# Later landings in the order of the instructions: 2.5 and 2.1 behind the shared bus, not 1.8 and 1.1

## The chip, the cores and the metric

The kernel runs on one core of a Trainium2 chip. The core has a matrix engine (PE in the profile, its weight loads PEld), a vector engine (DVE), a scalar engine (ACT), GpSimd (POOL), and a queue that only issues DMAs (SP). Each has a queue of its own that is worked off in the order in which the program was written; semaphores hold an instruction back until its data are there. The metric is the device time of one execution in microseconds (us). Before the change the median of three runs is 2048.77 us (2047.79 to 2051.46).

## What is computed

One step of a one-layer streaming encoder, for a prompt of 1024 tokens and 8 samples of 16 new tokens each, 1152 tokens together, with 1024 channels:

```python
h = rmsnorm(x)
qa, ka, va, qi, ki, wi, qb, kb, vb, gb, bb, ab, ga, gbr = split(h @ w_in)
# A: an indexer picks top-k keys for each query, then softmax attention with a relative bias
oa = dsa(qa, qi, wi, k_all, v_all, ki_all, topk, rel_bias)
# B: short causal convolution, then the gated delta rule in chunks
ob = rmsnorm(gated_delta(conv(qb), conv(kb), conv(vb), g, beta, state)) * silu(gb)
x = x + (sigmoid(ga) * (oa @ w_proj_a) + sigmoid(gbr) * (ob @ w_proj_b)) @ w_out
u_gate, u_val = split(rmsnorm(x) @ w_up)
x = x + (gelu(causal_dwconv(u_gate)) * u_val) @ w_down
x = x + sigmoid(rmsnorm(x) @ w_ple_gate) * (p @ w_ple)
y = rmsnorm(x)
```

The samples attend to a cache of 256 past keys each beside their new ones, and carry on a delta-rule state and two convolution states. All these states are outputs too.

## The kernel before

**The work.** Activations lie with channels on the partitions and tokens along the free axis, in three blocks of 384 tokens. Every product with a weight is made of three matmuls: activations and weights are split into a high part (`H`, `wh`) and a low part (`L`, `wl`), and `wh`·`H`, `wh`·`L` and `wl`·`H` are added up in PSUM. A dense job (`_Job`) is one tile of 128 output channels: its weight tile is loaded (`wr`), split (`weights`, `part`), multiplied block by block into a bank (`dense`), and evacuated (`evac`).

**The stages.**

1. *Mixers.* `norm1`, then the dense projections of `w_in`. In between go the indexer (`indexer`), the search for the top-k threshold (`topk_rows`, on ACT and DVE), the local part of the delta rule (`gdn_local`), its scan over the chunks (`gdn_scan`), the prompt's attention (`attention`, three workers) and that of the samples (`samples`). `jpp` and `jb` are dense jobs for `w_ple` and `w_proj_b` that run in the same stage.
2. *Merge.* `ja` (`w_proj_a`), which needs the attention of prompt and samples, and `jo` (`w_out`).
3. *Up-projection* in 22 tiles (`_Up`), with seven half-size products in place of eight, convolution, gelu, product.
4. *Down-projection* in the same manner, the gate of the per-layer embedding (`jd`), the last norm.

**What sets the order.** The order of all queues is made by a planner in the program, `_Driver`. Each piece of work is a generator, a thread. It yields what it needs next: an engine (`PE`, `ACT`, `DVE`, `POOL`, `SP`), an event of another thread, a buffer of a bank of buffers (`_Banks`), or `DMA`, the landing of its own transfers. The planner holds a clock for each engine and a time for each thread. In `run` it takes, again and again, the thread that can start first (then the one of the smallest number for its priority) and lets it issue its next instructions. So the planned times appear nowhere in the program but as the order of the instructions in the queues. `dense` has priority 9, the last: dense matmuls go where nothing else can start earlier.

`note` advances the clocks by a cost that `cost` gives for each operation. A DMA (engine `SP`) takes 0.46 us of SP's clock, its transfer is put behind all others on one shared bus (`self.bus`, from 0.2 us after the issue), and the thread's landing time `th.dma` is the bus's time plus a constant, one for loads (source in DRAM) and one for stores. The transfer's own time is 0.05 us plus, for each row, 0.0025 us or its bytes over 360 GB/s, whichever is more. DMAs that ACT issues for an evacuation (`own`) are noted as SP's too.

The landing time is read at four places: a thread that yields `DMA` goes on at that time (`_start`); `give` marks a buffer free not before it; `stored` sets an event at it; and threads for a landing (`arrival`, `landed`, `down_split`) are handed it. The real wait is a semaphore that is set when the transfer has landed, whatever the planner thought; a wait that the planner does not know of, such as one for a tile that is used again with no bank around it, is kept by semaphores alone.

**The threads that the prediction speaks of.**

- `gdn_chain` (two of them) goes through 8 chunks of the prompt. For each it loads `x` and `r`, yields `DMA`, and makes some matmuls with DVE steps between them. `gdn_norm` goes through the chunks behind it: load `sg`, transpose, yield `DMA`, multiply, store to `obT`.
- `samples` starts after `gdn_scan` has ended. `attn_cache` loads for each of 8 batches a selector (`x` from `selM` into an `evo` buffer) and then four tiles of cached keys (`skr`), each time: take one of two buffers, issue, yield `DMA`. `attn_samples` (two of them, four batches each) splits each key tile (`skH`, `skL`), multiplies, takes the softmax (`sz`), multiplies by the values (`sv`), and after four batches by the new values (`svN`, with `szn`) and stores to `oaT`.
- `merge_loads` loads `oaT` and `obT` back into `L` and splits them into `H` and `L`, as inputs of `ja` and `jb`. The third block of `ja` waits for the store of the samples (`sdone`).
- `mixers` ends with `drv.run(*self.samples(s3), *ev, self.jb[-1].done)`: the merge's threads are made only after samples, attention and `jb` have been placed.
- `evo` is a bank of four buffers of 128x384, used by most evacuations, by attention's outputs and value loads, by the samples, and for the gates that `jb` loads ahead of each block (`pre_gate`).

Of the kernel before, what the change touches and what calls it, by code (L numbers as in the profile page):

```python
# [87 lines left out]
class _Driver:  # L88
# [33 lines left out]
    def note(self, e, cost, port=False, load=False):  # L122
        th = self.cur
        if th.eng == e and cost < 0.1:
            cost += self.OWN[e]
        s = max(self.clk[e], th.t if th.eng in (e, None) else th.t + self.LAT)
        if port:
            s = max(s, self.port[POOL if e == DVE else DVE])
            self.port[e] = s + cost
        self.clk[e] = s + cost  # L130
        if e == SP:
            self.bus = max(self.bus, s + 0.2) + cost
            self.clk[e] = s + 0.46
            th.dma = max(th.dma, self.bus + (1.8 if load else 1.1))
        else:
            th.t, th.eng = s + cost, e

# [3418 lines left out]
```

## Time and profile before

| | |
|---|---|
| median of three runs | 2048.77 us |
| lowest and highest | 2047.79, 2051.46 us |
| the profiled execution | 2047.44 us, its span 2045.6 us |
| mean granted clock of the matrix engine | 0.996 |
| busy: PE, DVE, ACT, POOL | 2009.0, 1530.1, 1024.2, 650.1 us |
| DMA, mean over the span | 172 GB/s |

The profile's span runs from the first to the last instruction of the program; the time of the execution has 1.84 us around it. A row of instructions names engine, operation, and output <- inputs by the program's tile names; buffer numbers are left out, so `evo` is any of the four. All instructions bear the line L192, that of the helper which records them, so the tile names tell them apart. In the list of waits a row has who waited, for what, us in total, times, and the longest.

### The profile page before, as it was taken

What the parts mean: (1) busy time and instruction counts of PE and PEld (TensorE: products, weight loads), DVE (VectorE), ACT (ScalarE), POOL (GpSimd) and SP (SyncE); (2) the same over time, 40 slices, a digit from 0 to 9 for tenths busy, and PEclk for the clock granted to TensorE, in tenths of its full rate; (3) what the DMA queues carried; (4) which work ended last, traced back from release to release, by engine and by line L of the source; (5) the groups of instructions that cost most, each with busy time, mean ns of one, the idle gap of its engine ahead of it and who ended that gap; (6) DMA issues with size and microseconds to landing.
All of it is one profiled execution on the core that took longest, in us unless ns stands there. A gap on an engine that the chain in (4) does not pass through costs nothing.

```text
span 2045.6 us, 37985 instructions
## 1 busy us (share of the span) xinstructions
PE 2009.0 (98%) x13440; PEld 1961.5 (96%) x13440; DVE 1530.1 (75%) x3708; ACT 1024.2 (50%) x2061; POOL 650.1 (32%) x871
## 2 busy tenths in 40 slices
PE   7999999999999999999999999999999999999998
PEld 6899999999999998989999999999999999999998
DVE  7278989988664777778655788787788786657797
ACT  5267667656644555576423344333343354434454
POOL 2244543432223434454354322111221210112322
PEclk9999999999999999999999999999999999999999
DMA  7443356766528574477575433434465366656463
GB/s 277 115 126 97 91 193 199 221 194 175 155 78 247 171 220 143 143 232 218 174 241 168 148 120 122 151 118 156 154 210 193 131 221 221 213 164 209 150 198 127
DMA packets 264014, 352.02 MB, mean 172 GB/s; under 512 B 43324, under 2 KB 207504, under 8 KB 263696
## 3 DMA queue, kind: packets, MB, share of 16 engines
q1 hardware_dynamic: 241024, 323.11, 50.5%
q10 hardware_dynamic: 22800, 26.49, 3.8%
q8 instruction: 106, 1.74, 0.4%
q14 instruction: 84, 0.69, 0.1%
HBM read 241.07 MB, written 110.08 MB: 172 GB/s over the span
## 4 chain that ended last, share of the span: by engine, by line
PE 88%; DVE 3%; DMA 3%; issue 1%; ACT 1%; SPq 0%; POOL 0%; ACTq 0%; DVEq 0%; POOLq 0%
PE up L192 36%; PE acc L192 35%; PE at L192 7%; PE dn L192 5%; PE gd L192 3%; PE ix L192 1%; DMA ppT<-evo 1%; PE rp L192 1%; DVE z L192 0%; DMA sg<-sgb 0%; SPq L192 0%; DMA obT<-sg 0%; DVE e L192 0%; DVE SC L192 0%; PE ixs L192 0%
## 5 line engine op out<-in xcount | busy, mean ns | idle before, releaser
L192 PE MATMUL acc<-H,wh 128*128 128x384 f32 (+1 forms) x1328 | 468.9, 353 | 3.1 <-ACT evo L192 3.0
L192 PE MATMUL acc<-H,wl 128*128 128x384 f32 (+1 forms) x1328 | 450.1, 339 | 0.5 <-POOL wl L192 0.5
L192 PE MATMUL acc<-L,wh 128*128 128x384 f32 (+1 forms) x1328 | 449.7, 339 | 0.0
L192 POOL TENSOR_TENSOR wl<-wr,wh 128x256 fp32r<-128x256 f32 (+1 forms) x255 | 220.4, 886 | 447.6 <-ACT wh L192 388.6
L192 PEld LDWEIGHTS acc<-H,wh 128*128 128x128 f32 x1328 | 250.4, 189 | 10.2 <-ACT evo L192 4.1
L192 PE MATMUL up<-B,wh 128*128 128x288 f32 x1272 | 257.1, 296 | 0.0
L192 PEld LDWEIGHTS acc<-L,wh 128*128 128x128 f32 x1328 | 250.6, 189 | 3.3
L192 PEld LDWEIGHTS acc<-H,wl 128*128 128x128 f32 x1328 | 249.9, 188 | 2.2 <-POOL wl L192 1.0
L192 PE MATMUL up<-T,wh 128*128 128x288 f32 x1012 | 243.4, 295 | 0.0
L192 PEld LDWEIGHTS up<-B,wh 128*128 128x128 f32 x1272 | 204.1, 188 | 0.0
L192 PE MATMUL up<-B,wl 128*128 128x288 f32 x636 | 187.9, 295 | 0.0
L192 PEld LDWEIGHTS up<-T,wh 128*128 128x128 f32 x1012 | 174.2, 188 | 0.1
L192 ACT CAST wh<-wr 128x1024 fp32r<-128x1024 f32 (+3 forms) x133 | 113.1, 851 | 116.8 <-PE acc L192 42.7
L192 POOL TENSOR_TENSOR ssq<-ssq,sqs 128x384 f32<-128x384 f32 (+1 forms) x69 | 70.5, 1024 | 166.7 <-ACT sqs L192 160.0
L192 PEld LDWEIGHTS up<-B,wl 128*128 128x128 f32 x636 | 119.4, 188 | 0.0
L192 ACT ACTIVATE ja<-SC,cola 128x768 bf16<-128x768 f32 (+2 forms) x93 | 96.8, 1041 | 25.4 <-DVE cola L192 19.1
L192 ACT CAST wh<-s 128x512 fp32r<-128x512 f32 x88 | 52.5, 619 | 102.7 <-PE up L192 97.0
L192 ACT COPY u<-up 128x576 f32<-128x576 f32 x64 | 40.9, 640 | 102.5 <-PE up L192 102.1
L192 PE MATMUL up<-T0L,wh 128*128 128x288 f32 x296 | 87.4, 295 | 0.3 <-DVE T0L L192 0.3
L192 DVE TENSOR_TENSOR wl<-s,wh 128x512 fp32r<-128x512 f32 x75 | 56.6, 762 | 41.3 <-ACT wh L192 40.9
L192 PE MATMUL up<-T0H,wh 128*128 128x288 f32 x296 | 87.4, 295 | 0.0
L192 PE MATMUL up<-T0H,wl 128*128 128x288 f32 x296 | 87.1, 294 | 0.0
(537 smaller groups left out, 5302.4 us busy)
## 6 DMA issues: line engine op xcount, KB each, us to landing
wr<-in_w_in SPq DMA_DIRECT2D x47, 512.0 KB, 3.9
AT<-fv SPq DMA_DIRECT2D x22, 576.0 KB, 3.1
wr<-in_w_up SPq DMA_DIRECT2D x22, 512.0 KB, 4.5
gates<-evo ACTq DMA_DIRECT2D x48, 192.0 KB, 3.3
xs<-in_w_down SPq DMA_DIRECT2D x48, 192.0 KB, 3.5
S<-xs SPq DMA_DIRECT2D x48, 192.0 KB, 4.0
qkv<-evo SPq DMA_DIRECT2D x36, 192.0 KB, 3.6
T<-AT SPq DMA_DIRECT2D x11, 576.0 KB, 3.9
```

The costliest lines, as they stand in the source:

```text
L192: r = f(*a, **k)
```

## The change

The two constants behind the bus become 2.5 us for a load and 2.1 us for a store, where they were 1.8 and 1.1. Nothing else is touched: no cost, no buffer, no thread, no instruction.

```diff
@@ -131,7 +131,7 @@
         if e == SP:
             self.bus = max(self.bus, s + 0.2) + cost
             self.clk[e] = s + 0.46
-            th.dma = max(th.dma, self.bus + (1.8 if load else 1.1))
+            th.dma = max(th.dma, self.bus + (2.5 if load else 2.1))
         else:
             th.t, th.eng = s + cost, e
```

## The prediction

> **What bounds the kernel now.** I read the page first, then the stretches of the span, then what the PE queue waited for.
>
> ```profile
> span 2045.6 us, 37985 instructions
> PE 2009.0 (98%) x13440; PEld 1961.5 (96%) x13440; DVE 1530.1 (75%) x3708; ACT 1024.2 (50%) x2061; POOL 650.1 (32%) x871
> PE 88%; DVE 3%; DMA 3%; issue 1%; ACT 1%; SPq 0%; POOL 0%; ACTq 0%; DVEq 0%; POOLq 0%
> ...
> 800.00:900.00 100.00, 93.79 (x629) 89.12 (x627) 71.00 (x218) 62.53 (x145) 49.90 (x74) 1.00 0.61 180
> 900.00:1000.00 100.00, 97.24 (x668) 92.60 (x667) 80.36 (x265) 66.82 (x167) 46.72 (x81) 1.00 0.66 201
> 1000.00:1020.00 20.00, 20.00 (x135) 19.97 (x134) 9.37 (x24) 4.78 (x12) 6.54 (x10) 1.00 0.62 188
> 1020.00:1040.00 20.00, 20.00 (x115) 20.00 (x114) 6.79 (x13) 4.34 (x8) 5.89 (x7) 1.00 0.87 273
> 1040.00:1200.00 160.00, 159.66 (x945) 159.19 (x944) 110.32 (x185) 63.08 (x126) 70.63 (x60) 1.00 0.52 164
> 1200.00:1900.00 700.00, 700.00 (x5282) 699.78 (x5281) 534.51 (x914) 288.30 (x473) 123.26 (x167) 1.00 0.52 172
> 1900.00:2045.60 145.60, 139.87 (x878) 139.06 (x876) 115.23 (x240) 71.78 (x124) 40.47 (x37) 0.97 0.48 158
> ```
>
> In the stretches the first pair is the window and its length, then busy time (and count) of PE, weight loads, DVE, ACT, POOL, then the granted clock and DMA. TensorE is the bound, at the full clock. The order of its queue can win at most 2045.6 - 2009.0 = 36.6 us, and from 1000 to 1900 us there is nothing to win: 0.3 us of idle time in all. Idle time lies in the mixers, where small products of attention and of the delta rule share the queue with the dense projections. That is where a planner's idea of a DMA's landing matters, because there it decides whether a small product or a dense one goes next. What PE waited for, over the whole span:
>
> ```profile
> PE ac L192 <- ACT H L192: 6.7, 1, 6.7
> PE at L192 <- DVE sg L192: 3.7, 2, 2.3
> PE acc L192 <- ACT evo L192: 3.0, 2, 1.9
> PE at L192 <- DMA evo<-vTs: 2.2, 2, 1.5
> ...
> PE gd L192 <- DMA vc<-qkv: 1.2, 1, 1.2
> ...
> PE at L192 <- DMA x<-qkv: 1.0, 1, 1.0
> ```
>
> The first is the start, before any matmul. The three that name a DMA are loads which came after the point where the order had put their product. The two behind `sg` belong with them: in 795 to 825 us DVE sat 3.0 us for the load of `sg` and PE 2.3 us for DVE.
>
> ```profile
> DVE sg L192 <- DMA sg<-sgb: 3.0, 1, 3.0
> ...
> PE at L192 <- DVE sg L192: 2.3, 1, 2.3
> ```
>
> **The change, part by part.** No instruction is added or removed. Every work thread that yields DMA is put back into the order 0.7 us later behind a load and 1.0 us later behind a store, and so is a buffer that is given back after its store. The instructions, their buffers and their semaphores stay; only places in the five queues move. What was planned and what was measured (KB each, median from issue to landing):
>
> ```profile
> gates<-evo ACTq DMA_DIRECT2D x48, 192.0 KB, 3.3
> evo<-gates SPq DMA_DIRECT2D x24, 192.0 KB, 2.4
> pbT<-evo SPq DMA_DIRECT2D x24, 192.0 KB, 2.7
> skr<-in_ckT SPq DMA_DIRECT2D x32, 128.0 KB, 2.3
> sg<-sgb SPq DMA_DIRECT2D x9, 256.0 KB, 2.8
> obT<-sg SPq DMA_DIRECT2D x9, 256.0 KB, 3.1
> ...
> skr<-kTs SPq DMA_DIRECT2D x32, 8.0 KB, 2.3
> ```
>
> By the code a 192 KB store counts 0.2 + 0.6 of bus + 1.1 = 1.9 us, and 2.9 after; the rows say 2.7 and 3.3, so the stores get nearer. A 192 KB load counts 2.6 and then 3.3, against 2.4 for `evo<-gates`; `sg` counts 0.2 + 1.3 + 1.8 = 3.3 and then 4.0, against 2.8; the second half of `skr` 2.4 and then 3.1, against 2.3. So many loads, and those of the long chains among them, get counted too late.
>
> The Trainium skill, page "DMA: Bandwidth & Descriptors", section "Anatomy of one DMA", puts one DMA at 2.0 us plus its bytes over 436 GB/s, a fit for the GpSimd path; as an estimate that is 2.3 us for 128 KB and 2.45 us for 192 KB. The trace agrees with it at 2.3 and 2.4 us. By this rule the load half of the change leads away from the chip, its gain below would shrink to that of the store alone (1 us), and the sum would be 10 - 1 = 9 us slower; by the rows that PE waited for, it is the one worked out now.
>
> *The gain.* Six late loads hold PE: two of `evo<-vTs`, one of `vc`, one of `x`, two behind `sg`. Each product now goes 0.7 us later with dense matmuls ahead of it: 6 x 0.7 = 4.2 us. The longest wait of `acc<-ACT evo`, 1.9 us, has an evacuation behind buffers whose stores had not landed; 1.0 of it may go. That makes 5.2; since the order moves everywhere and a new order has late loads of its own, I take 4. Bounds: 0, and all six waits with that evacuation, 3.7 + 2.2 + 1.2 + 1.0 + 1.9 = 10.0.
>
> *The loss.* Dense matmuls are the filler, and the filler ends. The samples' attention is one chain of loads: a selector and four key tiles for each of 8 batches, 40 times load, wait, next. It cannot start before the delta rule has finished, which has 8 loads of `x` in a row and 5 of `sg` after them. And the merge is not built before samples, attention and the projections `jb` are all placed. Rows of three views: loads by tile (shortest, median, longest issue in ns, first and last start), then SP's own queue in order of time.
>
> ```profile
> L192 SPq DMA_DIRECT2D x<-qkv x36: 359/462/1013, 615.1 to 755.8; - x36
> ...
> L192 SPq DMA_DIRECT2D sg<-sgb x9: 360/365/539, 697.4 to 822.9; - x9
> ...
> L192 SPq DMA_DIRECT2D skr<-in_ckT x32: 328/424/1822, 837.0 to 999.2; - x32
> ...
> 856.24 0.43 SPq L192 DMA_DIRECT2D skr<-in_ckT  x1
> ...
> 866.08 0.33 SPq L192 DMA_DIRECT2D skr<-in_ckT  x1
> ...
> 968.20 1.82 SPq L192 DMA_DIRECT2D skr<-in_ckT  x1
> ...
> 984.91 0.45 SPq L192 DMA_DIRECT2D skr<-in_ckT  x1
> ```
>
> From 968.20 to 984.91 lies one batch: 16.7 us for 5 waits, 3.3 us each, about what the planner counts for a pair of loads (0.2 + 0.4 + 0.4 + 1.8 = 2.8, more with others on the bus). There the chain is nothing but planned latency, and each wait grows by 0.7. From 856.24 to 866.08 one step took 9.8 us: there it waited for something else, and growth is absorbed. Over all, 40 steps fill 837.0 to 999.2, 4.1 us each; 3.3 of 4.1 would be 80%, and with the long steps off I let 70% of the growth count: 40 x 0.7 x 0.7 = 20 us. Ahead of it come 13 x 0.7 = 9 us of the delta rule. The end of the samples is planned 29 us later against the dense work; bounds 9 (samples' growth all absorbed) and 9 + 28 = 37.
>
> What covers it:
>
> ```profile
> L192 PE MATMUL at<-szn,svN x16: 270/275/275, 1001.0 to 1017.9; 128*128 128x128 f32 x16
> ...
> L192 SPq DMA_DIRECT2D oaT<-oS x2: 370/536/702, 1003.0 to 1019.1; - x2
> ...
> L192 SPq DMA_DIRECT2D pbT<-evo x13: 319/320/437, 1004.6 to 1033.8; - x13
> ...
> L192 ACT CAST H<-L x6: 508/512/515, 1009.1 to 1028.9; 128x384 fp32r<-128x384 f32 x6
> ...
> 1018.17 21.91 PE acc L192 x124
> ```
>
> The last product of the samples is at 1017.9. Their result is stored at 1019.1, loaded again and split until 1028.9 plus 0.5 and a subtraction, 1030. The last `pbT` goes out at 1033.8, so some 15 us of `jb` remain on PE behind the samples, and they hide just that way round of 11 us. With the samples 29 us later against the dense work, these 15 us are spent before the samples end: 14 us of the planner's time have no filler, and the way round stands open too, less the first products of `ja`, which need no samples (24 matmuls at 21.91 / 124 = 0.177 us, 4 us). The chip will not lose 14 + 11 - 4 = 21: SP does not wait for one landing before it issues the next load, the loads land in 2.3 where 3.1 is counted, and softmax and products get through faster with no dense matmul ahead of them. I take half, 10 us; bounds 0 (growth under 15) and 37 - 15 + 11 - 4 = 29.
>
> *Nothing* is put down for three stretches. The local part of the delta rule (up to 590.0 in the row below) is hidden by the top-k thread, whose DVE and ACT steps run to 607 and beyond with no DMA in them; if that cover were gone, three loads and two stores in a row would add 3 x 0.7 + 2 x 1.0 = 4 us for each of four heads.
>
> ```profile
> L192 DVE TENSOR_SCALAR Z<-gd x24: 272/285/417, 426.5 to 590.0; 32x128 f32<-32x128 f32 x16, 64x256 f32<-64x256 f32 x8
> ...
> L192 DVE TENSOR_SCALAR_CACHE_REDUCE MB<-MB x6: 553/886/1220, 524.2 to 607.1; 128x384 bf16<-128x384 bf16 x1, 128x512 bf16<-128x512 bf16 x1, 128x640 bf16<-128x640 bf16 x1, 128x768 bf16<-128x768 bf16 x1
> ```
>
> The up-projection (1200 to 1900) has PE at 700.00 of 700.00; its loads are asked for a whole tile ahead. Behind 1900 us PE is idle for 5.7 us, and no wait that names a DMA lies there; if one came, it would be one late load, 0.7 us.
>
> *Sum:* 2045.6 - 4 + 10 = 2051.6 of span. The profiled execution took 2047.4, 1.8 above its span, and the median of the runs is 1.3 above that: **2054.8**, say 2055.
>
> **Rivals.**
>
> *The chain is absorbed, faster.* If the samples' steps wait for their two tile buffers and for DVE and ACT (80.36 busy of 100 between 900 and 1000 us) and not for the counted landing, the shift stays under 15 us and `jb` still covers it. Then the gain stands alone, 4 to 10 us: 2039 to 2045, middle 2043. For it speaks the step of 9.8 us; against it the batch of 16.7 us.
>
> *It orders the same thing.* Dense matmuls are always ready, so 0.7 us is four of them; if the queues keep what they start from, or if gain and loss are of one size, nothing shows: 2049. For it speaks that six of seven measured waits are under 2 us; against it that nearly all orders of buffers and DMA change at once.
>
> *The buffers bind, slower by more.* `evo` has four buffers for attention, samples, `jpp` and `jb`. Each is now counted 1.7 us longer for a load and a store. If `jb` in the plan then stands for buffers, dense work is left over while the samples' selector load also waits for one, and the 29 us bound of the loss comes in: 2049 + 29 - 10 = 2068. It decides once three `jb` blocks in flight and one attention output hold all four.
>
> **How the numbers follow.** The three runs of this kernel lie 3.7 us, 0.2%, apart (2047.79 to 2051.46), so less than that either way can't be told from no change. Forecast, slower by 2 to 13 us: 0.40, with its own range 2051 to 2062; absorbed and faster: 0.29; the same order or a balance: 0.23; buffers bind: 0.08. Of the forecast's 0.40 some 0.06 lie within 4 us, and of the faster case 0.02; that gives faster 0.27, same 0.31, slower 0.42. The range for 8 in 10 runs from 2040 to 2066: below it lies the far half of the full gain, above it the bound where buffers bind.
>
> **What the changed profile would show.** The gain: the rows of PE for `evo<-vTs`, `vc`, `x` and `sg` shrink from 8.1 us together to under 5. The loss: the last `szn` product comes 10 us or more behind the last dense matmul of `jb`, and a stretch near 1020 to 1045 shows PE idle, waiting for the samples' softmax or for `H` of `oaT`. If the last `szn` still has `jb` behind it, the chain was absorbed and the forecast falls. Stretches behind 1200 us should differ by under 1 us; if they carry the difference, the whole reasoning is wrong.

## The result and the profile after

| | before | after |
|---|---|---|
| median of six runs each | 2048.76 us | 2063.53 us |
| lowest and highest | 2043.86, 2051.46 | 2061.69, 2065.22 |
| the profiled execution, its span | 2047.44, 2045.6 | 2064.63, 2062.8 |
| mean granted clock of PE | 0.996 | 0.991 |

The ratio is 1.0073, 95% interval 1.0059 to 1.0086: slower by 14.8 us. (In two of the experiments below, e2 and e11, one execution of twelve took some 5070 us in a slow state; it counts in the median given there, but not in the ratio.) The profiled executions lie 17.2 us apart, and it is these 17.2 that the traces can explain. First the page of the kernel after:

```profile
span 2062.8 us, 38000 instructions
...
PE 2018.2 (98%) x13440; PEld 1967.5 (95%) x13440; DVE 1540.8 (75%) x3706; ACT 1028.7 (50%) x2069; POOL 643.7 (31%) x861
...
PEclk9999999999999999999989999999999999999999
...
PE 90%; DVE 4%; DMA 3%; issue 1%; SPq 1%; ACT 0%; POOL 0%; DVEq 0%; POOLq 0%; ACTq 0%
```

PE executes the same 13440 matmuls and is busy 9.2 us longer, 2018.2 against 2009.0; its idle time, span less busy time, grows by 8.0, from 36.6 to 44.6. One slice of the clock, the 21st, 1031 to 1083 us, is no longer 9. The stretches tell where. Rows of the kernel after: window and length, then busy time (and count) of PE, weight loads, DVE, ACT and POOL, then granted clock, DMA share, GB/s:

```profile
100.00:1000.00 900.00, 889.36 (x5674) 853.77 (x5672) 714.37 (x2177) 554.47 (x1252) 383.20 (x556) 1.00 0.57 172
...
1000.00:1020.00 20.00, 19.42 (x124) 18.62 (x124) 8.01 (x22) 4.07 (x10) 4.91 (x12) 1.00 0.79 232
1020.00:1040.00 20.00, 12.65 (x58) 11.42 (x56) 4.21 (x13) 3.03 (x8) 2.00 (x3) 0.66 0.23 69
1040.00:1060.00 20.00, 14.61 (x68) 13.78 (x66) 8.31 (x13) 5.20 (x10) 6.42 (x6) 0.83 0.53 170
1060.00:1080.00 20.00, 19.31 (x110) 18.71 (x110) 11.48 (x19) 6.03 (x11) 13.20 (x12) 1.00 0.69 207
1080.00:1100.00 20.00, 18.72 (x106) 18.04 (x105) 12.33 (x19) 7.45 (x12) 12.15 (x12) 1.00 0.75 232
1100.00:1200.00 100.00, 98.94 (x572) 98.36 (x571) 66.44 (x117) 37.46 (x80) 33.96 (x30) 1.00 0.43 138
1200.00:1900.00 700.00, 699.31 (x5273) 698.57 (x5272) 536.19 (x924) 289.20 (x476) 113.07 (x155) 1.00 0.51 170
```

The same first stretch of the kernel before:

```profile
100.00:1000.00 900.00, 881.12 (x5639) 844.85 (x5637) 704.68 (x2192) 550.32 (x1247) 375.83 (x557) 1.00 0.57 170
```

- 100 to 1000 us: PE idle 10.6 us where it was 18.9. This is **the gain, 8.2 us**, and 35 more matmuls are done by then. How firm is such a number? Two runs of the experiments below have the same queues up to the merge, e7 as before and e9 as after: there PE idles 19.5 and 12.3 us. So one profile is good to 1 or 2 us here, and the gain is 7 to 8.
- 1000 to 1200 us: idle 0.6 + 7.4 + 5.4 + 0.7 + 1.3 + 1.1 = 16.4 where it was 0.3. This is **the loss, 16.0 us of idle time**.
- On top of it the granted clock falls where PE is idle. As an estimate, busy time at a clock of 0.66 and 0.83 costs (1 - 0.66) x 12.65 + (1 - 0.83) x 14.61 = **6.8 us more**.
- 1200 to 1900 us: 0.7 us.

That makes -8.2 + 16.0 + 6.8 + 0.7 = 15.3 of 17.2. The rest is small and spread, and stays open.

What PE waited for in the kernel after, over the whole span (who waited, for what: us in total, times, longest):

```profile
PE acc L192 <- ACT H L192: 5.7, 2, 5.0
PE at L192 <- DVE skL L192: 4.8, 2, 2.5
PE at L192 <- DVE sg L192: 2.2, 1, 2.2
PE at L192 <- DMA evo<-vTs: 2.2, 3, 1.2
PE at L192 <- ACT sz L192: 2.1, 1, 2.1
...
PE gd L192 <- DMA vc<-qkv: 0.9, 1, 0.9
```

The wait for `x` and the 3.0 us for `evo` are gone, and the four kinds named as the gain are down from 8.1 to 5.3. New at the top are `H`, `skL` and `sz`. They stand together in PE's timeline (start, us, operation, in brackets the idle time before it and who ended it):

```profile
1020.84 0.33 PE L192 MATMUL acc<-H,wl 128*128 128x384 f32 x1
1023.47 0.37 PE L192 MATMUL at<-skL,sbH 128*128 128x272 f32 x1 [2.30 <-DVE skL L192]
...
1026.54 0.56 PE L192 MATMUL at<-skL,sbH 128*128 128x272 f32 x1 [2.46 <-DVE skL L192]
...
1029.68 0.69 PE L192 MATMUL at<-c,sz 128*128 128x128 f32 x2 [2.13 <-ACT sz L192]
...
1031.05 3.63 PE L192 MATMUL at<-evo,sv 128*128 128x32 f32 x16 [0.46 <-ACT evo L192]
1034.48 2.05 PE L192 MATMUL at<-szn,svN 128*128 128x128 f32 x8
1036.19 0.67 PE L192 MATMUL acc<-H,wh 128*128 128x384 f32 x1
...
1037.83 0.34 PE L192 MATMUL acc<-H,wl 128*128 128x384 f32 x1
...
1045.29 0.69 PE L192 MATMUL acc<-H,wh 128*128 128x384 f32 x1 [5.00 <-ACT H L192]
1046.37 0.69 PE L192 MATMUL acc<-L,wh 128*128 128x384 f32 x1 [0.39 <-POOL L L192]
...
1050.70 0.52 PE L192 MATMUL acc<-H,wl 128*128 128x384 f32 x1
1051.02 0.49 PE L192 MATMUL acc<-H,wh 128*128 128x384 f32 x1
1051.34 0.35 PE L192 MATMUL acc<-L,wh 128*128 128x384 f32 x1
1051.52 0.34 PE L192 MATMUL acc<-H,wl 128*128 128x384 f32 x1
```

The matmul at 1020.84 is the last of `jb`. After it PE has nothing but the samples' last two key tiles, their softmax and the products with the values, and waits for each step. The last `szn` products begin at 1034.48, then come 18 matmuls of `ja` (the prediction counted 24 that need no samples), then 5.0 us of waiting for `H`, the block of `oaT` that the samples have just written. In PE's queue 84 matmuls of `jb` stood behind the last `szn` product before; now there is none. Tiles of the kernel after (shortest, median, longest ns, first and last start):

```profile
L192 SPq DMA_DIRECT2D skr<-in_ckT x32: 327/426/584, 843.9 to 1022.9; - x32
...
L192 PE MATMUL at<-szn,svN x16: 271/348/561, 1015.5 to 1036.1; 128*128 128x128 f32 x16
```

The cached keys began at 837.0 and were last asked for at 999.2; now it is 843.9 and 1022.9. So the samples start 6.9 us later, and their chain of loads is 16.8 us longer. The chain of waits behind it:

```profile
1037.89 0.50 SPq L192
1040.87 3.84 DMA L<-oaT
1044.73 0.52 ACT H L192
1045.32 1.01 POOL L L192
```

Store, load back, split, low part: the way round through DRAM, 9.2 us from the last `szn` at 1036.1 to 1045.3, which `jb` used to cover, lies open. SP issues the store at 1037.47 and the first load back at 1040.87; in between it issues six loads of the merge (`tg`), and the load back then takes 3.84 us.

### The profile page after: what moved, and what is told of

It is laid out like the page before. It is cut to its first block, busy times and chain, and to the rows that moved or that the text cites. A ratio compares the mean times of both kernels' runs of the same rounds, so it can differ in the third digit from the quotient of the medians.

```text
span 2062.8 us, 38000 instructions
## 1 busy us (share of the span) xinstructions
PE 2018.2 (98%) x13440; PEld 1967.5 (95%) x13440; DVE 1540.8 (75%) x3706; ACT 1028.7 (50%) x2069; POOL 643.7 (31%) x861
## 4 chain that ended last, share of the span: by engine, by line
PE 90%; DVE 4%; DMA 3%; issue 1%; SPq 1%; ACT 0%; POOL 0%; DVEq 0%; POOLq 0%; ACTq 0%
PE acc L192 36%; PE up L192 35%; PE at L192 8%; PE dn L192 5%; PE gd L192 3%; PE ix L192 2%; SPq L192 1%; DMA obT<-sg 1%; PE ac L192 1%; DVE e L192 1%; PE rp L192 1%; DMA sg<-sgb 0%; DMA raw<-in_w_in 0%; DMA evo<-gates 0%; PE ixs L192 0%
## 5 line engine op out<-in xcount | busy, mean ns | idle before, releaser
L192 POOL TENSOR_TENSOR wl<-wr,wh 128x256 fp32r<-128x256 f32 (+1 forms) x249 | 215.1, 886 | 451.0 <-ACT wh L192 391.6
L192 ACT ACTIVATE ja<-SC,cola 128x768 bf16<-128x768 f32 (+2 forms) x93 | 96.7, 1040 | 17.2 <-DVE cola L192 7.1
```

The costliest lines, as they stand in the source:

```text
L192: r = f(*a, **k)
```

## The experiments

My theory was: the loss is the samples' chain of counted loads outgrowing the `jb` behind it; the gain ahead is real and smaller. Rivals: the buffers bind (counted stores), or the merge's own order loses the time. The experiments, e1 to e12, ran in three groups, each beside the kernel before on its chip (the comments in the edits name the runs): medians of before 2047.9 (the first four), 2049.03 (the next four) and 2048.91 us (the last four).

**Loads alone, stores alone.**

```diff
-            th.dma = max(th.dma, self.bus + (1.8 if load else 1.1))
+            th.dma = max(th.dma, self.bus + (2.5 if load else 1.1))   # e1
+            th.dma = max(th.dma, self.bus + (1.8 if load else 2.1))   # e2
```

> Loads at 2.5, stores at 1.1 as before. In PE's queue 15 matmuls of jb stand behind the last product of the samples (84 before, none after the change, where 21 other matmuls stand behind the last of jb). Theory (the chains of loads outlast the dense work, and the gain is spread over the mixers): 15 matmuls are 2.6 us, so the samples' softmax is covered again but the way of their result through DRAM, 11 us, is open less 2.6 and less the 3 us of ja that need no samples; a loss of 5 to 8 us against a gain of 4 to 8 us before 1000 us: 2045 to 2053. Rival (the store constant, which holds the evo buffers longer, makes the loss): nothing of the loss is left, 2041 to 2044.

> Loads at 1.8 as before, stores at 2.1. In PE's queue 252 matmuls of jb stand behind the last product of the samples, 44 us of cover where 11 are needed. Theory: no loss at the end of the samples; of the gain the part that comes from stores, 1 to 4 us: 2043 to 2049. Rival (the buffers bind: dense work is left over because it stood for evo buffers, and PE idles for it before): PE has 10 us or more of idle time between 850 and 1000 us and the time is 2058 or more.

Loads alone: 2062.46 us, ratio 1.0071 (1.0057 to 1.0084), the whole loss; my expectation was too low by more than 9 us. Stores alone: 2052.39 us, 1.0013 (1.0001 to 1.0025), 3 us above what I expected; where they are lost stays open. The last products of the samples in the kernel with stores alone:

```profile
L192 PE MATMUL at<-szn,svN x16: 270/275/275, 981.6 to 994.1; 128*128 128x128 f32 x16
```

They come 24 us earlier than before, with 252 matmuls of `jb` behind them, and the time is no better: the additional cover shows no gain. Counting stores later, which holds `evo` longer, costs at most 0.25%, and PE idles 2.5 us from 850 to 1000 us where the rival of the buffers asked for 10 or more: this rival falls. The load's constant is what costs.

The gain shows only with both. The stretch of 100 to 1000 us, loads alone first, then stores alone:

```profile
100.00:1000.00 900.00, 882.76 (x5612) 846.58 (x5611) 714.47 (x2184) 549.34 (x1243) 382.38 (x554) 0.99 0.56 169
```

```profile
100.00:1000.00 900.00, 882.07 (x5623) 843.17 (x5622) 714.29 (x2201) 553.66 (x1256) 385.08 (x559) 0.99 0.56 168
```

Idle for 17.2 and 17.9 us, against 18.9 and 19.5 in two profiles of the old queues and 10.6 and 12.3 in two of the new: alone, each lies within some 2 us of the old queues, little more than two profiles of one order differ by, and neither has more matmuls done by 1000 us (5612 and 5623, against 5639 before).

**Samples and delta rule apart.** Which threads count landings later is chosen by the name of the thread's generator (`own`), so that the constants can differ:

```diff
+        self.own = gen.__name__ in ('gdn_chain', 'gdn_norms', 'gdn_samples', 'gdn_out', 'attn_cache', 'attn_samples')
...
+            th.dma = max(th.dma, self.bus + ((1.8 if load else 1.1) if th.own else (2.5 if load else 2.1)))   # e3
+            th.dma = max(th.dma, self.bus + ((2.5 if load else 2.1) if th.own else (1.8 if load else 1.1)))   # e4
```

> 2.5 and 2.1 everywhere but in the delta rule's scan and the samples' attention with its loads of the cache, which keep 1.8 and 1.1. In PE's queue 33 matmuls of jb stand behind the last product of the samples, 5.8 us. Theory: the loss goes but for about 2 to 4 us of the way round, the gain of the rest stays: 2041 to 2048. Rival (the loss comes from somewhere else in the order, as of the top-k, the buffers or the merge): 2058 or more.

> 1.8 and 1.1 everywhere but in the delta rule's scan and the samples' attention with its loads of the cache, which get 2.5 and 2.1. 43 other matmuls stand behind the last of jb. Theory: the loss without most of the gain, idle time of PE between 1000 and 1060 us of 20 us or more and a lower granted clock there: 2066 to 2080. Rival: 2044 to 2054.

All later but these six: 2052.48 us, 1.0022 (1.0011 to 1.0032); some 10 of the 14.8 us are gone, though not all, and 4 us more are left than I expected. Only these six later: 2073.23 us, 1.0124 (1.0107 to 1.0141), more than the whole change. The samples' last products, in the first and in the second:

```profile
L193 PE MATMUL at<-szn,svN x16: 270/275/275, 1010.5 to 1028.1; 128*128 128x128 f32 x16
```

```profile
L193 PE MATMUL at<-szn,svN x16: 415/421/561, 1031.9 to 1048.5; 128*128 128x128 f32 x16
```

In the first, 33 matmuls of `jb` stand behind the last of them again. In the second they begin 12.4 us later than with the full change, and the full change is 9.7 us faster: with everybody counted late the samples fall back less against the rest than with them alone.

**Which of the two.** The same switch, for the cached keys alone (set at the start of `attn_cache`) and for the four generators of the delta rule alone:

```diff
+        self.drv.cur.own = True                                                                      # e5, in attn_cache
...
+        self.own = gen.__name__ in ('gdn_chain', 'gdn_norms', 'gdn_samples', 'gdn_out')              # e6
...
+            th.dma = max(th.dma, self.bus + ((2.5 if load else 2.1) if th.own else (1.8 if load else 1.1)))
```

> 1.8 and 1.1 everywhere but in the one thread that loads the cached keys and selectors, which gets 2.5. No matmul of jb stands behind the last product of the samples, 15 other matmuls stand behind the last of jb. Theory (40 counted waits of 0.7 us more are most of the shift): the loss at the end of the samples is there with little of the gain, 8 to 18 us: 2056 to 2066, with the granted clock down between 1020 and 1060 us. Rival (the shift comes from the delta rule's scan, which lies ahead of it): within 4 us of before.

> 1.8 and 1.1 everywhere but in the threads of the delta rule's scan, which get 2.5 and 2.1. 30 matmuls of jb stand behind the last product of the samples, where 84 do before. Theory: the samples begin some 9 us later and end some 9 us later; 30 matmuls are 5.3 us, the way round of 11 us is open less 5.3 and less 3 of ja: a loss of 0 to 4 us, 2048 to 2053. Rival: 2058 or more.

Cached keys alone: 2066.73 us, 1.0082 (1.0069 to 1.0095). Delta rule alone: 2053.36 us, 1.0019 (1.0008 to 1.003). So one generator with 40 waits for loads makes the loss by itself. Its loads, and the wait in PE's timeline that follows:

```profile
L192 SPq DMA_DIRECT2D skr<-in_ckT x32: 328/424/1419, 838.3 to 1025.9; - x32
...
1052.59 0.69 PE L192 MATMUL acc<-H,wh 128*128 128x384 f32 x1 [5.34 <-ACT H L192]
```

From the first to the last load it takes 187.6 us, where 162.2 were needed: 25.4 us more for 40 waits of 0.7 = 28. From 1000 to 1200 us PE idles 8.2 us, and a clock of 0.74 on 14.27 us of busy time from 1040 to 1060 us costs 3.7 more by the estimate above: 11.9 of the 19.3 us between the two spans. By 1000 us 5583 matmuls are done, against 5639 before, so some of the other 7.4 may lie ahead of that; no run shows it.

**The merge apart from the mixers.** The constants are switched where `merge_ffn` starts (`far`), the first pair in the mixers, the second behind:

```diff
+    far = 1.8, 1.1              # e7;   2.5, 2.1 in e8 and e9
...
+            th.dma = max(th.dma, self.bus + (self.far[0] if load else self.far[1]))
...
     def merge_ffn(self):
+        drv.far = 2.5, 2.1      # e7;   1.8, 1.1 in e8 and e9
```

In e8 the six generators above keep 1.8 and 1.1 besides; in e9 they don't.

> 1.8 and 1.1 in the mixers, so that all queues up to the merge are those of before; 2.5 and 2.1 from the merge on. Theory (the stalls of ja on tg, MH and wh come from the load constant in the merge's own threads, since they are in the run where scan and samples keep the old constants and not in the one where they alone are late): PE idle for 3 to 5 us in 1035 to 1110 us, 2050 to 2055. Rival (they are left over from the gap ahead of ja): 2046 to 2050, no idle time there.

> 2.5 and 2.1 in the mixers but for scan and samples, 1.8 and 1.1 there and from the merge on. Theory: what the third run still lost goes with the merge's stalls, some 4 us, and what the mixers gain, 0 to 4 us, shows: 2045 to 2050. Rival (no gain, and the loss of the third run lies ahead of the merge): 2051 to 2054.

> 2.5 and 2.1 in the mixers, scan and samples included, 1.8 and 1.1 from the merge on. In PE's queue no matmul of jb is left behind the samples' last product, as after the change. My theory (the loss is the samples' chain, and some 5 us of it the merge's own threads): if the two add, this is the change less what the merge alone cost (2055.2 against 2048.8, some 6 us): 2056 to 2060, with PE idle and the lower granted clock near 1020 to 1050 as after the change, and no wait above 1 us in jo. Rival (the merge's own late counts cost only when the samples are on time, since both waits overlap): 2061 to 2066, as after the change.

Later from the merge on: 2055.19 us, 1.0025 (1.0015 to 1.0036), 6.2 us lost with queues that are those of before up to the merge. Mixers later but the six: 2049.58 us, 0.9998 (0.9987 to 1.001), as before. Mixers later with the six: 2058.93 us, 1.0044 (1.0028 to 1.006), 4.6 us less than the full change. So the merge's part, 5 to 6 us, adds to the rest; the rival that both overlap (from 2061 us) is left only the last bit of the interval, 2048.9 x 1.006 = 2061.2. PE's waits from 1000 to 1210 us, later from the merge on:

```profile
PE acc L193 <- DVE tg L193: 1.8, 3, 0.7
PE acc L193 <- ACT MH L193: 0.7, 1, 0.7
PE acc L193 <- ACT wh L193: 0.6, 1, 0.6
...
PE acc L193 <- DVE ML L193: 0.4, 1, 0.4
```

These are the gated products and split weights of `ja` and `jo`, 3.5 us together, where before had 0.3 us of idle time in all. No run tells whether it is the weights' loads or the gates' that are put too late there, nor where the other 2.7 us of the median lie.

**Taking the chain away.** The cached keys' loads are issued without waiting, in the plan, for one to land before the next is asked for; a thread for the arrival (there is one in the program) sets the event at the counted landing:

```diff
-                yield DMA
                 self.skv[b, k] = kr
-                self.drv.set(self.ske[b][k])
+                self.drv.spawn(self.arrival(self.ske[b][k], self.drv.cur.dma), 2)
```

This edit is put on the kernel after (e10), on the kernel before (e12), and on the one with 2.5 and 2.1 in the mixers but for the delta rule's four generators (e11).

> The change with one thing more: the samples' cached keys are issued without waiting in the plan for one to land before the next is asked for. My theory (it is the chain of 40 waits that grows): the chain's growth is gone and only the scan's remains; in PE's queue 15 matmuls of jb stand behind the samples' last product again instead of none: 2052 to 2060. Rival (the samples are late by SP's queue or by their two tile buffers, not by the counted landing): 2061 to 2066, as after the change.

> The kernel before with the cached keys issued without waiting and nothing else; 66 matmuls of jb stand behind the samples' last product where 84 did. My theory (cover of 66 is enough): 2046 to 2051, as before. Rival (the samples' end still sets the time before the change, so that issuing ahead gains): 2040 to 2045.

> A version that keeps the later counts only where no loss was seen: cached keys issued without waiting, 2.5 and 2.1 in the mixers but for the scan, 1.8 and 1.1 in the scan and from the merge on; 33 matmuls of jb stand behind the samples' last product. My theory (loss by the cover at the samples' end, gain of the rest too small to show): 2046 to 2053, not faster than before by more than can be told. Rival (the gain ahead of 1000 us is real, 5 us or more, once the loss is away): 2041 to 2045.

On the kernel after: 2054.11 us, 1.0026 (1.0015 to 1.0037); 9.4 of the 14.8 us are back, with the constants as changed and only the serial counting gone. Its samples and its longest wait behind the start:

```profile
L192 PE MATMUL at<-szn,svN x16: 270/275/275, 1003.9 to 1021.0; 128*128 128x128 f32 x16
```

```profile
PE acc L192 <- ACT H L192: 5.5, 2, 4.9
```

The samples end 15 us earlier, but only 15 matmuls of `jb`, 2.6 us at 0.175, stand behind them, so the way round still shows with 4.9 us.

On the kernel before the edit loses, against my expectation: 2053.81 us, 1.0022 (1.001 to 1.0034). Of the 5.9 us between the two spans 3.7 are idle time of PE ahead of 1000 us (22.6 against 18.9); why the new order idles there stays open. But the pair e12 and e10 has this edit on both sides and differs by the change alone: 2053.81 and 2054.11 us. With the serial counting away, the two constants make no difference that can be told, where they cost 14.8 us with it; the gain and the losses that remain cancel. On the third it wins a little: 2045.73 us, 0.9983 (0.9971 to 0.9994), the fastest of all, by an amount at the edge of what can be told. e11 and e12 differ by the later counts alone, 8.1 us, and here is their gain in PE's busy time of the same stretch, the one without later counts first:

```profile
100.00:1000.00 900.00, 877.44 (x5580) 841.18 (x5579) 695.72 (x2153) 541.64 (x1221) 376.66 (x557) 1.00 0.57 171
```

```profile
100.00:1000.00 900.00, 887.30 (x5653) 851.12 (x5653) 714.51 (x2184) 552.65 (x1248) 383.04 (x561) 0.99 0.57 171
```

Idle time falls from 22.6 to 12.7 us, as it fell from 18.9 to 10.6 by the change itself. So the gain is real and shows once the loss is away. The mixers later but the six (e8) also lost some idle time there, 18.9 to 14.5 us, and did not become faster: in that profile the granted clock is 0.994 in place of 0.996, and only 5612 matmuls are done by 1000 us, against 5639 before. What lowers the clock there stays open.

## Why the prediction was right, and where it was off

The forecast was slower, 2055, out of a gain of 4 and a loss of 10 us. The sign, the places and the chain behind them held. The time came out at 2063.5, inside the range, 1.5 us outside the forecast's own range. That it lies no farther off is in part luck: the gain was put too small by 4 us and the loss by 13 (16.0 + 6.8 against 10), and the two errors work against each other.

- **The shift of the samples: right.** Put at 29 us against the dense work, 9 from the delta rule and 20 from the cached keys. Measured: the start 6.9 later, the chain 16.8 longer, together 23.7; the last `szn` 18.2 later (1036.1 against 1017.9) and the end of `jb`, by the count of its matmuls in PE's queue, 11.9 earlier (1020.8 against 1032.7), so 30.1. The rows of issue times were enough for this, though one was misread: SP issues a selector 0.5 us ahead of the next key tile (984.44 and 984.91), so the 16.7 us taken for five waits of 3.3 us are four steps of 4.2 us on the chip.
- **"I take half, 10": too small, because a term was missing.** From the end of `jb` to the end of the way round PE idled 2.30 + 2.46 + 2.13 + 0.46 = 7.4 us for the samples and 5.00 + 0.39 = 5.4 on the way round, 12.7 together: more than the 10, and far from the 21 that were halved. The 14 us without filler in these 21 were not all idle time. Of the 15.3 us between the last matmul of `jb` and the last `szn` PE is busy for 7.9, nearly all of it with the samples' own products, which have to run in any case. What the prediction left out altogether is that PE goes on slower after such a gap: 6.8 us at a lower clock. That makes 19.5, close to the 21, but not for the reason that gave 21.
- **The gain: right in kind, half in size.** 4 us forecast, 8.2 of idle time measured, within its bounds of 0 to 10. The rows named for it fell from 8.1 to 5.3 and not under 5; the 3.0 us of `acc<-ACT evo` went too, and the rest lies in smaller waits. The Trainium skill's page "DMA: Bandwidth & Descriptors", section "Anatomy of one DMA", was weighed here: by its latency the load half leads away from the landings and only the store's 1 us is gained. Stores alone gave 1.0 us of idle time and loads alone 1.7, neither clear of the spread, but the two together 8.2. So the rule, applied to each count by itself, does not tell what an order gains.
- **Nothing for the rest: wrong for the merge.** The stretches behind 1200 us moved by 0.7 us, as forecast. But `ja` and `jo` are planned with the same constants, and the idle time in the merge, 16.4 - 0.6 (ahead of 1020 us) - 12.7 = 3.1 in the trace and 5 to 6 by the runs, was put at nothing without a word on it.
- **What was to show** did: the last `szn` 15.3 us behind the last dense matmul of `jb`, and PE idle from 1020 to 1045 us for softmax and for `H`. Not foreseen in this list were the waits for `skL`, the split of the last two key tiles: the chain's own loads, late as its softmax is.
- **The rivals.** Absorbed: refuted, the chain grew by 16.8 of the 28 us counted (40 x 0.7), a share of 0.6 where 0.7 was allowed. The same order: refuted, `jb` behind the samples went from 84 matmuls to none. Buffers: its 2068 is near in time, but no dense work is left over behind the samples, and stores alone leave the time at 2052.4, while the loads of the cached keys alone make the loss.

With 12.7 in place of 10, 8.2 in place of 4, and the two terms that it lacked, 6.8 for the clock and 3.1 for the merge, the prediction's own sum would have been 2045.6 - 8.2 + 12.7 + 6.8 + 3.1 = 2060.0, against a span of 2062.8.

## What to carry to other kernels

A planner's latency is multiplied by the longest row of waits that are planned one after the other: count the waits of each serial chain, and compare the growth with the filler that stands behind that chain's end. If the filler is spent, nothing in the queue is left to go into the gap, and it costs more than its idle time: here 12.7 us of idle time, and an estimated 6.8 us at a lower clock. Rather than tune the constant for all, take the serial waits out of the chain, and keep two constants where two stages answer in opposite ways: the run that did both was the fastest here, by 0.17% and at the edge of what can be told, while the serial waits taken out alone, with the old constants, lost 4.9 us.

## What the runs showed of the hardware

The granted clock was not expected to matter. Windows of 10 us of the kernel after, in the columns of the stretches above:

```profile
1020.00:1030.00 10.00, 3.12 (x15) 2.32 (x14) 2.93 (x9) 2.49 (x6) 2.00 (x3) 0.70 0.32 101
1030.00:1040.00 10.00, 9.54 (x45) 9.10 (x43) 1.28 (x4) 0.54 (x2) 0.00 (x0) 0.62 0.15 37
1040.00:1050.00 10.00, 4.61 (x14) 3.78 (x13) 1.68 (x2) 2.04 (x4) 1.96 (x2) 0.73 0.52 174
1050.00:1060.00 10.00, 10.00 (x55) 10.00 (x54) 6.63 (x11) 3.15 (x6) 4.46 (x4) 0.93 0.54 166
```

In the second window PE is busy 9.54 of 10 us and still has only 0.62. The same work in the kernel before:

```profile
1014.29 1.87 PE L192 MATMUL at<-evo,sv 128*128 128x32 f32 x16
...
1017.12 1.05 PE L192 MATMUL at<-szn,svN 128*128 128x128 f32 x8
```

After the change these take 3.63 and 2.05 us, 1.94 and 1.95 times as long, and dense matmuls start every 0.32 us (1050.70 to 1051.02) instead of 0.18 (1051.34 to 1051.52). In shorter windows of the same trace the granted clock has just two levels: 1.00 from 1020 to 1023 us, 0.50 from 1026.5 to 1037, 1.00 from 1037.7 to 1040.2, 0.50 from 1045.3 to 1051, and 1.00 from 1051.4 on. The values between them in the windows of 10 us are means over both.

- *Losing it.* The first gap of 2.30 us and the three short matmuls behind it, 0.6 us of work, were enough: from 1023.0 to 1024.2 us the clock is 0.93, from 1024.0 to 1026.5 it is 0.51. Of the three matmuls from 1023.47 the first takes 0.37 us, of those from 1026.54 it takes 0.56.
- *Getting it back.* It was full again from 1037.6 us, 6.6 us after PE went on at 1031.05 without another gap. The 5.0 us of waiting for `H` lost it once more, and it was back at 1051.3, 6.0 us after dense work went on at 1045.29.

The Trainium skill's page "TensorE: Matmul & The Clock Gate", in its part "The HAM clock gate", says that the clock is either half or full, that an idle window of about 3.4 us halves it and a busy one of that length restores it. The trace agrees with the two levels, at 0.50 and 1.00. The return took longer here, 6.6 and 6.0 us, and no single gap ahead of the first loss was as long as 3.4 us.
